# Three edits in a hybrid decoder layer: the w_down sums held until the rotary stage is done, six decay products given more PSUM banks, and the transition to the feed-forward part reordered

## The chip, the cores and the metric

The kernel runs on one core of a Trainium2 chip. The metric is the device time of one execution in microseconds (us); the median of several executions is compared. The engines of the core are TensorE (PE in rows: matmuls; PEld are its weight loads), VectorE (DVE), ScalarE (ACT), GpSimd (POOL) and SyncE (SP, which here only issues DMAs). Each engine works through its instructions in order. PSUM is the memory into which TensorE writes, in banks of 128 x 512 float32.

## What is computed

One layer of a decoder trunk on 1,040 positions (16 meta tokens and 1,024 inputs) of width 1,024, all in float32:

```python
u = rmsnorm(h, mix_norm)
proj = u @ w_in + b_in
aq, ak, av, gq, gk, gv, gr, g_low, gate_a, gate_b = split(proj)
aq, ak = rope(aq), rope(ak)
y_att = swa_attention(aq, ak, av, sinks)          # window of 128, 8 heads, 2 key heads
z = g_low @ w_alpha + b_alpha
log_a = log_sigmoid(z) / 16                       # decay of the linear attention
y_gla = rmsnorm(gla(gq, gk, gv, log_a)) * silu(gr)
h = h + (sigmoid(gate_a) * (y_att @ w_pa) + sigmoid(gate_b) * (y_gla @ w_pg)) @ w_out
u = rmsnorm(h, ffn_norm)
a, v = split(u @ w_up)
h = h + (gelu(causal_dwconv(a)) * v) @ w_down
out = rmsnorm(h, final_norm)[16:]
```

## The kernel before

**Matmuls in two parts.** Every large float32 operand is split into a high part (a cast on ScalarE, L72) and a low part (a subtraction on VectorE, L73). A product is then three matmuls: high x high, high x low, low x high (L91 to L93 in `dense`). A weight strip of 128 columns is loaded by SyncE (L80), split, and used for all positions in three chunks of columns; two strips' buffers alternate.

**Rotary stage.** The loop over j (4 for the keys, then 0 to 3 for the queries) computes a strip q_j, evacuates it on ScalarE into rt (L311, two buffers), copies it with its halves exchanged into rs (L317: four DMAs issued by ScalarE; rs has one buffer), multiplies rs on GpSimd (L318) and rt on VectorE (L319), and adds both into c1 (L330). Behind it come strips gk0, gk1 (keys of the linear attention), gates g0 to g3, gq0, then the first tm weights (token-major products tm0, one for each of nine position tiles, evacuated by VectorE into tv, L385), gq1, the second tm products tm1, and gates from g4 on.

**w_down sums.** The feed-forward products use a seven-product scheme of the Strassen kind, which needs sums of quarter blocks of the weights. For w_down they are made early: `tsum` is a step function that is called between chunks of the projections. Of each three calls one loads a 1 MB block into half of the tile tw (L415), one makes its four sums on VectorE (L421 to L424), and one stores it to the DRAM tile t_d (L418). There are eleven blocks, and tw holds two. Nothing in the data ties these steps to the rotary stage. tw lies in the pool buffer C2, which afterwards holds the tile at of the decay stage (cleared on GpSimd, L473).

**Decay stage.** From the transposed g_low (glT, filled tile by tile through the banks gp) six products z are made (two halves s, three chunks c0; L449), each evacuated twice: by VectorE into zt (L450) and by ScalarE into la (L451). The chain of exp, log and scan behind it ends in the first linear-attention products gm (L483). Banks have tags: "mm" three, "s" two, "pv" two, "pt" one.

**Transition.** The section under `manual_schedule` keeps the written order on its engines; elsewhere a scheduler orders instructions. There the last strip of the output projection (wo7) ends, the root of the mean square is taken for the second half of the positions (nt on TensorE, square root on ScalarE, reciprocal on VectorE, the diagonal matrices dg, and bc, their product with ones), `u2` scales the rows of hT with it (L896), and `op_hi` and `op_lo` split the rows into the operands B22, and after half-subtractions (L1177, L1188, L1191) T1 and T2 (L899, L902). `turn_strip` transposes a strip of hT (th) for its store. `product(n)` does product n of the feed-forward (L978 to L980), for even blocks in two halves of columns; `w_split(n)` makes its weights' parts on ScalarE (L964) and VectorE (L965); `madd` adds a product to an accumulator (L1168).

Of the kernel before, what the change touches and what calls it, by code (L numbers as in the profile page):

```python
# [8 lines left out]
F32 = mybir.dt.float32  # L9
# [37 lines left out]
def hybrid_block(ctx, tc, x, meta, mix_norm, w_in, b_in, w_alpha, b_alpha, sinks, ghn,  # L47
# [9 lines left out]
    def f32(ap):  # L57
        return ap.bitcast(F32)
# [8 lines left out]
    def bank(tag, name):  # L67
        return ps.tile([P, 512], F32, tag=tag, bufs=PB[tag], name=name)
# [337 lines left out]

    t_d = dp.tile([NPAIR, 4, P, 512], F32, name="t_d")
    tw = big.tile([P, 2, 4, 512], F32, tag="C2", name="tw")
    tcount = [0]

    def tsum(c0=0):
# [30 lines left out]
    tq = tm.tile([P, KT * 328], F32R, tag="tl", name="tq")  # L442
    la = f32(tb)[:, :2 * T].rearrange("p (s t) -> p s t", s=2)
    zt = f32(tq)[:, :2 * T].rearrange("p (s t) -> p s t", s=2)
    for s in range(2):
        ba = bcol[:, 29 + s:30 + s]
        for c0, n in CH_ALL:
            o = bank("s", f"z{s}_{c0}")
            pe.matmul(o[:, :n], wal[:, s * P:s * P + P], glT[:, c0:c0 + n], start=True, stop=True)  # L449
            dve.tensor_scalar(zt[:, s, c0:c0 + n], o[:, :n], ba, 0.0, ALU.add, ALU.min)  # L450
            act.activation(la[:, s, c0:c0 + n], o[:, :n], AF.Abs, bias=ba, scale=1.0)  # L451
# [424 lines left out]
    def turn_strip(ht, k, tag="pv"):  # L876
        tp = bank(tag, f"th1_{k}")
        for j in range(4):
            pe.transpose(tp[:, j * P:j * P + P], hT[:, k, 1, 2 + j * P:2 + j * P + P], ident)
        act.copy(ht[:, :, k * P:k * P + P], tp.rearrange("p (j n) -> p j n", j=4))  # L880
        if k % 4 == 3:
            c = k // 4 * 512
            sp.dma_start(h_d[4:8, :, c:c + 512].rearrange("j p n -> p j n"), ht[:, :, c:c + 512])
# [75 lines left out]
    def w_split(n):  # L959
        b, pn = seq[n]  # L960
        nm = SRC[pn]
        src = quarter(b, nm) if nm[0] == "A" else sums[b][nm]
        t = wp.tile([P, 2, 4, P], F32R, tag=("wst", "whi", "wlo")[n % 3], name=f"wq{n}")
        act.copy(t[:, 0], src)  # L964
        dve.tensor_tensor(t[:, 1], src, f32(t[:, 0]), ALU.subtract)  # L965
        slots[n] = t
# [123 lines left out]
    with tc.manual_schedule(engines={mybir.EngineType.PE, mybir.EngineType.DVE, mybir.EngineType.Activation,  # L1090
                                     mybir.EngineType.Pool}):
        wout(6, take("wo6_1"), (2,))
        turn_strip(hts[1], 5)
        w_split(0)
        w_split(3)
        w_last = take("wo7_1")
        w_split(1)
        w_split(2)
        o = dense(w_last, lambda k: mh[k // 4][:, k % 4, 514:1026], lambda k: ml[k // 4][:, k % 4, 514:1026], KT, 512,
                  "wo7_2")  # L1100
        turn_strip(hts[1], 6)
        hv = hT[:, 7, 1, 2:]
        dve.tensor_tensor(hv, hv, o, ALU.add)
        sq = p2.tile([P, 512], F32, tag="sg0", bufs=2, name="sq_last")
        act.activation(sq, hv, AF.Square)
        for b in range(2):
            sum_first(b, 1)
        op_tile(("B22",), big, "C1")
        op_tile(("T2",), big, "C2")
        op_tile(("T1",), b2, "E")  # L1110
        w_split(4)
        w_split(5)
        pr = {0: product(0)}


        nt = bank("pt", "nt")
        for j in range(4):
            pe.matmul(nt[:, j:j + 1], rs[1][:, 2 + j * P:2 + j * P + P], ones_m[:, 0:1], start=True, stop=False)
            pe.matmul(nt[:, j:j + 1], sq[:, j * P:j * P + P], ones_m[:, 0:1], start=False, stop=True)
        act.activation(rt4[:, 0], nt[:, 0:4], AF.Sqrt, bias=eps_c, scale=1.0)  # L1120
        dve.reciprocal(rt4[:, 1], rt4[:, 0])
        dg = p2.tile([P, 4, P], F32, tag="sg1", bufs=2, name="dg")
        for j in range(4):
            if j % 2:
                dve.tensor_scalar(dg[:, j], ident, rt4[:, 1, j:j + 1], None, ALU.mult)
            else:
                act.activation(dg[:, j], ident, AF.Identity, scale=rt4[:, 1, j:j + 1])
        bc = bank("pt", "bc")
        turn_strip(hts[1], 7)

        def spread():
            for j in range(4):
                pe.matmul(bc[:, j * P:j * P + P], ones_f, dg[:, j], start=True, stop=True)

        pr[1] = product(1, spread)
        p1a = b2.tile([P, HQ], F32, tag="rs1", name="p1_0")
        p1v = b2.tile([P, HQ], F32, tag="rs0", name="p1_1")
        keep_prod(0, p1a, pr[0])
        w_split(6)
        pr[2] = product(2)  # L1140
        w_split(7)
        p2.release()
        fp = tc.alloc_tile_pool(name="fp", bufs=1, reuse_waits="tile")
        aa0 = fp.tile([P, 2, HQ], F32, name="aa0")
        vt = fp.tile([P, 4, 4, P], F32, tag="S", bufs=1, name="vt").rearrange("p a k n -> p (a k n)")
        vt = vt[:, 0:1024].rearrange("p (a n) -> p a n", a=2)
        st_load(2)
        st_load(3)
        keep_prod(1, p1v, pr[2])
        pr[3] = product(3)  # L1150

        def lo22(k):
            op_lo("B22", k - 4, 1, hT[:, k:k + 1, 1])

        for k in range(4, 8):
            u2(k, 1, bc)
            op_hi("B22", k - 4, 1, hT[:, k:k + 1, 1])
            if k > 4:
                lo22(k - 1)
        lo22(7)  # L1160
        pr[4] = product(4)
        pr[5] = product(5)

        wk = hT.rearrange("p k h n -> p (k h n)")

        def madd(dst, src, prod, off):
            for o, a, m in prod:
                dve.tensor_tensor(dst[:, a - off:a - off + m], src[:, a - off:a - off + m], o[:, :m], ALU.add)  # L1168

        def half(k, hf):  # L1170
            return hT[:, k:k + 2, hf]

        madd(aa0[:, 0], p1a, pr[1], 0)
        for k in range(4):
            u2(k, 1, bc)
        for k in (0, 2):
            dve.tensor_tensor(half(k, 0), half(k, 1), half(k, 0), ALU.subtract)  # L1177
            op_hi("T1", k, 2, half(k, 0))
        w_split(8)
        for k in (0, 2):  # L1180
            op_lo("T1", k, 2, half(k, 0))
        madd(vt[:, 0], p1v, pr[3], 2)
        pr[6] = product(6)
        pr[7] = product(7)
        keep_prod(0, aa0[:, 1], pr[4])
        keep_prod(1, vt[:, 1], pr[5])
        for k in (0, 2):
            dve.tensor_tensor(half(k, 1), half(k + 4, 1), half(k, 1), ALU.subtract)  # L1188
        op_tile(("T3",), big, "B0")
        for k in (0, 2):  # L1190
            dve.tensor_tensor(half(k + 4, 1), half(k + 4, 1), half(k, 0), ALU.subtract)  # L1191
            op_hi("T2", k, 2, half(k + 4, 1))
        w_split(9)
        for k in (0, 2):
            op_lo("T2", k, 2, half(k + 4, 1))
            op_hi("T3", k, 2, half(k, 1))
        pr[8] = product(8)
        pr[9] = product(9)
        w_split(10)
        w_split(11)  # L1200
        for k in (0, 2):
            op_lo("T3", k, 2, half(k, 1))
        w_split(12)
        w_split(13)
        op_tile(("T4",), big, "B1")
        for k in (0, 2):
            dve.tensor_tensor(half(k + 4, 0), half(k + 4, 0), half(k + 4, 1), ALU.subtract)
            op_hi("T4", k, 2, half(k + 4, 0))
        madd(p1a, p1a, pr[8], 0)
        madd(p1v, p1v, pr[9], 2)  # L1210
        for k in (0, 2):
            op_lo("T4", k, 2, half(k + 4, 0))
        pr[10] = product(10)
        pr[11] = product(11)
        pr[12] = product(12)
        ca, cv, cv0 = whole(0, 1), whole(1, 1), whole(1, 0)
        act.copy(cv0[:, 0], vt[:, 0])
        w_split(14)
        madd(ca[:, 0], p1a, pr[10], 0)
        madd(ca[:, 1], ca[:, 0], pr[6], 0)  # L1220
        madd(aa0[:, 1], aa0[:, 1], pr[6], 0)
        w_split(15)
        pr[13] = product(13)
        madd(cv[:, 0], p1v, pr[11], 2)
        madd(cv[:, 1], cv[:, 0], pr[7], 2)
        madd(cv0[:, 1], vt[:, 1], pr[7], 2)
        sum_make(2)
        dve.tensor_tensor(aa0[:, 1], aa0[:, 1], p1a, ALU.add)
        w_split(16)
        conv(0, 0)  # L1230
        madd(ca[:, 0], ca[:, 0], pr[12], 0)
        conv(0, 1)
        w_split(17)
        dve.tensor_tensor(cv0[:, 1], cv0[:, 1], p1v[:, 0:512], ALU.add)
        madd(cv[:, 0], cv[:, 0], pr[13], 2)
# [215 lines left out]
```

## Time and profile before

| | |
|---|---|
| three runs | 1427.16, 1425.56, 1423.03 us; median 1425.56 |
| profiled execution | 1421.07 us, of which its span (first to last instruction) 1419.3 |
| TensorE | busy 1368.4 us, 96% of the span |
| VectorE, ScalarE, GpSimd | 64%, 41%, 29% |
| mean granted clock of TensorE | 0.983 |

The durations below come from the one profiled execution. The granted clock is given as a share of full speed; its two levels are 1.2 GHz (0.50) and 2.4 GHz (1.00), and a value between them is a mean over a stretch. An engine's idle time costs something only if TensorE waits at the end of it.

### The profile page before, as it was taken

The page shows a single profiled execution, that of the slowest core. Times are in us where ns is not written, and L with a number is a line of the kernel's source. Part 1 is how long each engine was busy: PE and PEld are TensorE (multiplying, and loading weights), DVE is VectorE, ACT ScalarE, POOL GpSimd, SP SyncE. Part 2 cuts the span into 40 slices and gives each one's busy share as a digit, 9 for nine tenths or more (in the row PEclk, how much of TensorE's full clock was granted, in tenths as well). Part 3 has the DMA queues.
Part 4 walks back from the last instruction along what each step waited for, and adds up shares of the span by engine and source line. Part 5 has one row for each costly group of instructions (what it writes and reads, how often), then busy time and mean ns, then how long its engine had stood idle before and what let it go on. Part 6 is the DMA issues. An engine that isn't in the chain of part 4 may idle for free.

```text
span 1419.3 us, 21786 instructions
## 1 busy us (share of the span) xinstructions
PE 1368.4 (96%) x8235; PEld 1244.9 (88%) x8235; DVE 911.1 (64%) x1467; ACT 582.6 (41%) x1145; POOL 416.5 (29%) x289
## 2 busy tenths in 40 slices
PE   6979999989999999999998999999999999999998
PEld 6979999878988988999987888899999888888886
DVE  6566211566677877444467998877676777766674
ACT  6313211535454556443353533333333333654452
POOL 0211110012122221224221387667656652100000
PEclk9989999999999999999999999999999999999999
DMA  7789811122322224555332033233233225975543
GB/s 219 214 250 315 250 44 57 45 71 70 87 70 73 67 73 131 167 168 168 90 134 90 0 127 112 97 112 110 83 112 111 75 97 205 348 262 194 192 151 119
DMA packets 161351, 190.24 MB, mean 134 GB/s; under 512 B 19050, under 2 KB 115110, under 8 KB 161238
## 3 DMA queue, kind: packets, MB, share of 16 engines
q1 hardware_dynamic: 158150, 180.25, 40.4%
q10 hardware_dynamic: 3088, 8.51, 1.9%
q8 instruction: 68, 1.11, 0.3%
q14 instruction: 45, 0.37, 0.1%
HBM read 133.33 MB, written 52.74 MB: 131 GB/s over the span
## 4 chain that ended last, share of the span: by engine, by line
PE 69%; DVE 5%; DMA 2%; ACT 2%; issue 1%; SPq 0%; DVEq 0%; ACTq 0%
PE m L979 10%; PE m L978 10%; PE m L980 10%; PE dn L1376 5%; PE dn L1377 5%; PE dn L1375 5%; PE d_g L91 3%; PE d_g L92 3%; PE d_g L93 3%; PE d_wo L91 2%; PE d_wo L93 2%; PE d_wo L92 2%; PE d_pj L91 2%; PE d_pj L92 2%; PE d_pj L93 2%
## 5 line engine op out<-in xcount | busy, mean ns | idle before, releaser
L979 PE MATMUL m<-op_T,wq 128*128 128x258 f32 (+2 forms) x528 | 170.9, 324 | 5.5 <-DVE op_T L902 5.5
L978 PE MATMUL m<-op_T,wq 128*128 128x258 f32 (+2 forms) x528 | 170.7, 323 | 0.8 <-ACT op_T L899 0.8
L980 PE MATMUL m<-op_T,wq 128*128 128x258 f32 (+2 forms) x528 | 170.1, 322 | 0.0
L91 PE MATMUL d_g<-uh,hi_g 128*128 128x342 f32 x480 | 159.1, 332 | 2.4 <-PEq L571 2.4
L92 PE MATMUL d_g<-ul,hi_g 128*128 128x342 f32 x480 | 156.7, 326 | 2.4 <-issue 2.4
L93 PE MATMUL d_g<-uh,lo_g 128*128 128x342 f32 x480 | 156.5, 326 | 0.0
L979 PE MATMUL m<-op_B,wq 128*128 128x256 f32 (+2 forms) x396 | 127.1, 321 | 0.8 <-DVE op_B L902 0.6
L978 PE MATMUL m<-op_B,wq 128*128 128x256 f32 (+2 forms) x396 | 127.0, 321 | 0.0
L980 PE MATMUL m<-op_B,wq 128*128 128x256 f32 (+2 forms) x396 | 126.4, 320 | 0.0
L979 PEld LDWEIGHTS m<-op_T,wq 128*128 128x128 f32 x528 | 101.3, 192 | 14.1 <-DVE op_T L902 6.4
L964 ACT CAST wq<-S 128x512 fp32r<-128x512 f32 x80 | 49.4, 622 | 148.7 <-PE m L980 127.2
L978 PEld LDWEIGHTS m<-op_T,wq 128*128 128x128 f32 x528 | 101.0, 191 | 9.0 <-ACT op_T L899 1.2
L980 PEld LDWEIGHTS m<-op_T,wq 128*128 128x128 f32 x528 | 101.3, 192 | 7.8
L965 DVE TENSOR_TENSOR wq<-st,wq 128x512 fp32r<-128x512 f32 x72 | 84.8, 1183 | 28.9 <-ACT wq L964 28.9
L91 PEld LDWEIGHTS d_g<-uh,hi_g 128*128 128x128 f32 x480 | 92.7, 193 | 6.4 <-issue 2.8
L93 PEld LDWEIGHTS d_g<-uh,lo_g 128*128 128x128 f32 x480 | 92.7, 193 | 3.2 <-issue 3.1
L92 PEld LDWEIGHTS d_g<-ul,hi_g 128*128 128x128 f32 x480 | 92.8, 193 | 0.5 <-issue 0.4
L1046 POOL TENSOR_TENSOR hT<-hT 128x1024 f32<-128x1024 f32 x22 | 58.8, 2674 | 84.4 <-DVE hT L994 81.9
L979 PEld LDWEIGHTS m<-op_B,wq 128*128 128x128 f32 x396 | 74.9, 189 | 7.2 <-DVE op_B L902 1.2
L978 PEld LDWEIGHTS m<-op_B,wq 128*128 128x128 f32 x396 | 74.8, 189 | 5.8
L980 PEld LDWEIGHTS m<-op_B,wq 128*128 128x128 f32 x396 | 74.8, 189 | 5.8
L965 DVE TENSOR_TENSOR wq<-S,wq 128x512 fp32r<-128x512 f32 x80 | 68.0, 851 | 11.9 <-ACT wq L964 11.2
(345 smaller groups left out, 3682.9 us busy)
## 6 DMA issues: line engine op xcount, KB each, us to landing
st<-in_w_up_dram SPq DMA_DIRECT2D x22, 1024.0 KB, 7.8
stage<-g_d SPq DMA_DIRECT2D x77, 256.0 KB, 4.6
tw<-in_w_down_dram SPq DMA_DIRECT2D x11, 1024.0 KB, 8.4
t_d<-tw SPq DMA_DIRECT2D x11, 1024.0 KB, 5.1
stage<-t_d SPq DMA_DIRECT2D x44, 256.0 KB, 3.5
gate_d<-gev SPq DMA_DIRECT2D x60, 171.0 KB, 2.9
st_g<-in_w_in_dram SPq DMA_DIRECT2D x20, 512.0 KB, 3.8
g_d<-hT SPq DMA_DIRECT2D x11, 768.0 KB, 6.0
```

The source lines that it names most:

```text
L91: pe.matmul(o[:, :n], hi[:, k, :], rh(k), start=(k == 0), stop=False)
L92: pe.matmul(o[:, :n], hi[:, k, :], rl(k), start=False, stop=False)
L93: pe.matmul(o[:, :n], lo[:, k, :], rh(k), start=False, stop=(k == nk - 1))
L964: act.copy(t[:, 0], src)
L965: dve.tensor_tensor(t[:, 1], src, f32(t[:, 0]), ALU.subtract)
L978: pe.matmul(o[:, :m], t[:, 0, k], bh[:, k, a:a + m], start=(k == 0), stop=False)
L979: pe.matmul(o[:, :m], t[:, 0, k], bl[:, k, a:a + m], start=False, stop=False)
L980: pe.matmul(o[:, :m], t[:, 1, k], bh[:, k, a:a + m], start=False, stop=(k == 3))
L1046: pool.tensor_tensor(v, v, wk[:, 1028 + f * 1024:2052 + f * 1024].rearrange("p (h n) -> p h n", h=2), ALU.mult)
L1375: pe.matmul(o, gh[:, ts], dh, start=first, stop=False)
L1376: pe.matmul(o, gh[:, ts], dl, start=False, stop=False)
L1377: pe.matmul(o, gl[:, ts], dh, start=False, stop=last_)
```

## The change

Part A puts two copies of one column from c1, which is complete only after the last rotary add, into the two halves of tw. All loads into tw come after them. Part B takes the banks of the six z from a list. Part C moves the root's work between the two halves of product 0, the transposes of strips 6 and 7 behind product 0, bc ahead of product 1, product 2 forward, u2 and the split of B22 ahead of the weight splits 5, 6 and 7, the half-subtractions ahead of the first `madd`, and the weight splits 8 and 9 behind the second.

```diff
     tw = big.tile([P, 2, 4, 512], F32, tag="C2", name="tw")
+    for z in range(2):
+        dve.tensor_copy(tw[:, z, 0, 0:1], c1[:, 3, 0:1])
     tcount = [0]
...
+    zb = ["s", "pv", "s", "pv", "pt", "s"]
     for s in range(2):
         ba = bcol[:, 29 + s:30 + s]
         for c0, n in CH_ALL:
-            o = bank("s", f"z{s}_{c0}")
+            o = bank(zb.pop(0), f"z{s}_{c0}")
...
-        turn_strip(hts[1], 6)
...
         w_split(4)
-        w_split(5)
-        pr = {0: product(0)}
         nt = bank("pt", "nt")
+        dg = p2.tile([P, 4, P], F32, tag="sg1", bufs=2, name="dg")
+        def roots():
+            for j in range(4):
+                pe.matmul(nt[:, j:j + 1], rs[1][:, 2 + j * P:2 + j * P + P], ones_m[:, 0:1], start=True, stop=False)
+                pe.matmul(nt[:, j:j + 1], sq[:, j * P:j * P + P], ones_m[:, 0:1], start=False, stop=True)
+            act.activation(rt4[:, 0], nt[:, 0:4], AF.Sqrt, bias=eps_c, scale=1.0)
+            dve.reciprocal(rt4[:, 1], rt4[:, 0])
...
+        pr = {0: product(0, roots)}
+        turn_strip(hts[1], 6)
+        turn_strip(hts[1], 7)
+        bc = bank("pt", "bc")
         for j in range(4):
...
-        bc = bank("pt", "bc")
-        turn_strip(hts[1], 7)
-        def spread():
-            for j in range(4):
-                pe.matmul(bc[:, j * P:j * P + P], ones_f, dg[:, j], start=True, stop=True)
-        pr[1] = product(1, spread)
+            pe.matmul(bc[:, j * P:j * P + P], ones_f, dg[:, j], start=True, stop=True)
+        pr[1] = product(1)
...
+        pr[2] = product(2)
+        for k in range(4, 8):
+            u2(k, 1, bc)
+            op_hi("B22", k - 4, 1, hT[:, k:k + 1, 1])
+            if k > 4:
+                lo22(k - 1)
+        lo22(7)
+        w_split(5)
+        for k in range(4):
+            u2(k, 1, bc)
         w_split(6)
-        pr[2] = product(2)
         w_split(7)
...
-        madd(aa0[:, 0], p1a, pr[1], 0)
-        for k in range(4):
-            u2(k, 1, bc)
         for k in (0, 2):
             dve.tensor_tensor(half(k, 0), half(k, 1), half(k, 0), ALU.subtract)
             op_hi("T1", k, 2, half(k, 0))
-        w_split(8)
+        madd(aa0[:, 0], p1a, pr[1], 0)
         for k in (0, 2):
             op_lo("T1", k, 2, half(k, 0))
         madd(vt[:, 0], p1v, pr[3], 2)
+        w_split(8)
+        w_split(9)
...
-        w_split(9)
```

In the changed kernel the lines behind the edits stand two to six lower (L421 is L423, L449 is L452, L896 is L899, L902 is L905, L965 is L968, L1168 is L1174, L1177 is L1180).

VectorE in the rotary stage before (rt0 to rt3 and rs0 to rs3 belong to the four query strips; lo_ names the low part of a weight strip, tw the w_down block):

```order
L319 TENSOR_TENSOR rt0_444<-rt0_444,cs_224 128x1026
L73 TENSOR_TENSOR lo_q3_636<-st_q3_634,hi_q3_635 128x1024
L330 TENSOR_TENSOR c1_428<-rt0_444,rs0_445 128x1026
L421 TENSOR_TENSOR tw_835<-tw_835 128x512
L422 TENSOR_TENSOR tw_835<-tw_835 128x512
L423 TENSOR_TENSOR tw_835<-tw_835 128x512
L319 TENSOR_TENSOR rt1_538<-rt1_538,cs_224 128x1026
L73 TENSOR_TENSOR lo_gk0_730<-st_gk0_728,hi_gk0_729 128x1024
L330 TENSOR_TENSOR c1_428<-rt1_538,rs1_539 128x1026
L424 TENSOR_TENSOR tw_835<-tw_835 128x512
L421 TENSOR_TENSOR tw_835<-tw_835 128x512
L422 TENSOR_TENSOR tw_835<-tw_835 128x512
```

and the same place in the changed kernel:

```order
L73 TENSOR_TENSOR lo_q3_636<-st_q3_634,hi_q3_635 128x1024
L330 TENSOR_TENSOR c1_428<-rt0_444,rs0_445 128x1026
L319 TENSOR_TENSOR rt1_538<-rt1_538,cs_224 128x1026
L73 TENSOR_TENSOR lo_gk0_730<-st_gk0_728,hi_gk0_729 128x1024
L330 TENSOR_TENSOR c1_428<-rt1_538,rs1_539 128x1026
L319 TENSOR_TENSOR rt2_632<-rt2_632,cs_224 128x1026
L73 TENSOR_TENSOR lo_gk1_882<-st_gk1_880,hi_gk1_881 128x1024
L330 TENSOR_TENSOR c1_428<-rt2_632,rs2_633 128x1026
L319 TENSOR_TENSOR rt3_726<-rt3_726,cs_224 128x1026
L73 TENSOR_TENSOR lo_g0_966<-st_g0_964,hi_g0_965 128x1024
L330 TENSOR_TENSOR c1_428<-rt3_726,rs3_727 128x1026
L410 COPY tw_835<-c1_428 128x1 x2
```

The sums that stood between the rotary operations stand behind the last of them, and behind the new copies; all other rows keep their order.

TensorE in the decay stage before (z0 and z1 are the two halves, the number behind is the chunk; gp8 is the last transpose of g_low; d_g4 is gate strip g4):

```order
L394 MATMUL gp8_2251<-ident_73,tv1_8_2248 16x128
L449 MATMUL z0_0_2256<-glT_831,wal_829 128x272
L449 MATMUL z0_272_2260<-glT_831,wal_829 128x384
L93 MATMUL d_g4_14_2319<-uh_78,lo_g4_1880 128x342
L91 MATMUL d_g4_14_2319<-uh_78,hi_g4_1879 128x342
L92 MATMUL d_g4_14_2319<-ul0_79,hi_g4_1879 128x342
L93 MATMUL d_g4_14_2319<-uh_78,lo_g4_1880 128x342
L449 MATMUL z0_656_2264<-glT_831,wal_829 128x384
L91 MATMUL d_g4_14_2319<-uh_78,hi_g4_1879 128x342
L449 MATMUL z1_0_2268<-glT_831,wal_829 128x272
L92 MATMUL d_g4_14_2319<-ul0_79,hi_g4_1879 128x342
L93 MATMUL d_g4_14_2319<-uh_78,lo_g4_1880 128x342
```

and in the changed kernel, from the end of the last tm product on:

```order
L452 MATMUL z0_272_2262<-glT_831,wal_829 128x384
L452 MATMUL z1_0_2270<-glT_831,wal_829 128x272
L394 MATMUL gp8_2253<-ident_73,tv1_8_2250 16x128
L452 MATMUL z0_0_2258<-glT_831,wal_829 128x272
L452 MATMUL z0_656_2266<-glT_831,wal_829 128x384
L452 MATMUL z1_272_2274<-glT_831,wal_829 128x384
L452 MATMUL z1_656_2278<-glT_831,wal_829 128x384
L91 MATMUL d_g4_14_2321<-uh_78,hi_g4_1881 128x342
L92 MATMUL d_g4_14_2321<-ul0_79,hi_g4_1881 128x342
L93 MATMUL d_g4_14_2321<-uh_78,lo_g4_1882 128x342
```

The six z, which were spread among matmuls of g4, stand in one run ahead of g4, with gp8 among them.

VectorE in the transition before (wq4 to wq8 are the weight splits of products 4 to 8; op_B22 and op_T1 are low parts of operands; aa0 is the first madd):

```order
L1121 RECIPROCAL rt4_115<-rt4_115 128x4
L1125 TENSOR_SCALAR dg_8719<-ident_73,rt4_115 128x128 x2
L965 TENSOR_TENSOR wq6_8766<-s1t_8246,wq6_8766 128x512
L965 TENSOR_TENSOR wq7_8782<-s1t_8246,wq7_8782 128x512
L896 SCALAR_TENSOR_TENSOR hT_6649<-hT_6649,ccol_104,bc_8724 128x512 x2
L902 TENSOR_TENSOR op_B22_8673<-hT_6649,op_B22_8673 128x514
L896 SCALAR_TENSOR_TENSOR hT_6649<-hT_6649,ccol_104,bc_8724 128x512
L902 TENSOR_TENSOR op_B22_8673<-hT_6649,op_B22_8673 128x514
L896 SCALAR_TENSOR_TENSOR hT_6649<-hT_6649,ccol_104,bc_8724 128x512
L902 TENSOR_TENSOR op_B22_8673<-hT_6649,op_B22_8673 128x514 x2
L1168 TENSOR_TENSOR aa0_8789<-p1_0_8762,m1_0_8732 128x258
L1168 TENSOR_TENSOR aa0_8789<-p1_0_8762,m1_258_8749 128x256
```

and in the changed kernel from the reciprocal on:

```order
L1124 RECIPROCAL rt4_115<-rt4_115 128x4
L1127 TENSOR_SCALAR dg_8676<-ident_73,rt4_115 128x128 x2
L899 SCALAR_TENSOR_TENSOR hT_6651<-hT_6651,ccol_104,bc_8730 128x512 x2
L905 TENSOR_TENSOR op_B22_8669<-hT_6651,op_B22_8669 128x514
L899 SCALAR_TENSOR_TENSOR hT_6651<-hT_6651,ccol_104,bc_8730 128x512
L905 TENSOR_TENSOR op_B22_8669<-hT_6651,op_B22_8669 128x514
L899 SCALAR_TENSOR_TENSOR hT_6651<-hT_6651,ccol_104,bc_8730 128x512
L905 TENSOR_TENSOR op_B22_8669<-hT_6651,op_B22_8669 128x514 x2
L968 TENSOR_TENSOR wq5_8790<-st01_8247,wq5_8790 128x512
L899 SCALAR_TENSOR_TENSOR hT_6651<-hT_6651,ccol_104,bc_8730 128x512 x4
L968 TENSOR_TENSOR wq6_8797<-s1t_8248,wq6_8797 128x512
L968 TENSOR_TENSOR wq7_8800<-s1t_8248,wq7_8800 128x512
```

The splits wq6 and wq7, and wq5 (which stood just before the reciprocal), are now behind the low parts of B22. Behind the rows of the second list follow the half-subtractions, aa0, the low parts of T1, vt, and only then wq8 and wq9.

## Rows read from the trace of the kernel before

**Rows 1.** waits of TensorE over the whole span: us in total, times, longest
```profile
PE m L979 <- DVE op_T L902: 5.5, 3, 3.1
...
PE gm L483 <- DVE tq L496: 1.5, 2, 0.9
```

**Rows 2.** timeline of VectorE: start, us, line, op, out<-in [idle before <-releaser]
```profile
77.13 0.69 DVE L421 TENSOR_TENSOR tw<-tw 128x512 f32<-128x512 f32 x1 [10.62 <-DMA tw<-in_w_down_dram]
...
83.55 1.22 DVE L330 TENSOR_TENSOR c<-rt,rs 128x1026 f32<-128x1026 f32 x1
```

**Rows 3.** timeline of ScalarE, rotary stage; ACTq is its queue, here issuing copies
```profile
84.85 4.28 ACTq L317 DMA_DIRECT2D rs<-rt  x4
89.18 1.42 ACT L311 ACTIVATE rt<-d_q,ccol 128x258 f32<-128x258 f32 x3 [17.58 <-DMA rs<-rt]
...
101.29 2.45 ACTq L317 DMA_DIRECT2D rs<-rt  x4
```

**Rows 4.** timeline of GpSimd, rotary stage
```profile
95.60 3.40 POOL L318 TENSOR_TENSOR rs<-rs,sn 128x1026 f32<-128x1026 f32 x1 [15.51 <-DMA rs<-rt]
106.97 3.40 POOL L318 TENSOR_TENSOR rs<-rs,sn 128x1026 f32<-128x1026 f32 x1 [7.98 <-DMA rs<-rt]
```

**Rows 5.** timeline of TensorE, first matmuls of gk0 and of tm_0
```profile
89.71 0.59 PE L91 MATMUL d_gk<-uh,hi_gk 128*128 128x272 f32 x1 [8.36 <-ACT rt L311]
...
171.94 0.31 PE L381 MATMUL tm<-th,uh 128*16 128x328 f32 x1
```

**Rows 6.** table by stretches; columns stand in its first line
```profile
core 0: us, PE busy (x) PEld busy (x) DVE busy (x) ACT busy (x) POOL busy (x), PEclk, DMA share, GB/s
90.00:100.00 10.00, 10.00 (x52) 10.00 (x52) 4.50 (x2) 2.02 (x4) 3.40 (x1) 0.75 1.00 338
120.00:140.00 20.00, 20.00 (x129) 20.00 (x129) 10.90 (x18) 9.93 (x17) 0.00 (x0) 1.00 1.00 314
180.00:200.00 20.00, 20.00 (x136) 20.00 (x135) 2.50 (x5) 2.62 (x14) 4.17 (x14) 1.00 0.10 32
```

**Rows 7.** timeline of SyncE's queue, rotary stage
```profile
85.40 3.15 SPq L418 DMA_DIRECT2D t_d<-tw  x2
```

**Rows 8.** issues of the w_down loads: min/median/max, first and last start
```profile
L415 SPq DMA_DIRECT2D tw<-in_w_down_dram x11: 367/451/1155, 39.1 to 157.6; - x11
...
DMA to landing us min/median/max: 6.1/8.4/10.7
```

**Rows 9.** timeline of TensorE, decay products
```profile
251.00 1.37 PE L449 MATMUL z<-glT,wal 16*128 16x272 f32 x4
...
256.29 2.92 PE L449 MATMUL z<-glT,wal 16*128 16x384 f32 x4
```

**Rows 10.** table by stretches, decay products (columns as in rows 6)
```profile
255.00:256.00 1.00, 1.00 (x6) 0.92 (x5) 0.50 (x1) 0.70 (x2) 0.00 (x0) 0.74 0.00 0
256.00:262.00 6.00, 6.00 (x16) 4.01 (x15) 1.24 (x2) 2.75 (x5) 0.00 (x0) 0.50 0.01 3
```

**Rows 11.** timeline of VectorE, transition to feed-forward
```profile
758.10 1.40 DVE L896 SCALAR_TENSOR_TENSOR hT<-hT,ccol,bc 128x512 f32<-128x512 f32 x2
...
771.92 0.69 DVE L965 TENSOR_TENSOR wq<-st,wq 128x512 fp32r<-128x512 f32 x1 [1.63 <-ACT wq L964]
772.53 2.36 DVE L902 TENSOR_TENSOR op_T<-hT,op_T 128x1028 fp32r<-128x1028 f32 x2
...
809.63 0.68 DVE L965 TENSOR_TENSOR wq<-S,wq 128x512 fp32r<-128x512 f32 x1
```

**Rows 12.** timeline of TensorE, transition to feed-forward
```profile
752.74 0.36 PE L978 MATMUL m<-op_B,wq 128*128 128x258 f32 x1
...
754.26 1.05 PE L1133 MATMUL bc<-dg,ones_f 128*128 128x128 f32 x8
...
773.81 0.39 PE L979 MATMUL m<-op_T,wq 128*128 128x258 f32 x1 [3.14 <-DVE op_T L902]
...
811.23 0.28 PE L980 MATMUL m<-op_T,wq 128*128 128x258 f32 x1
```

More of the change, by code (lines that the diff above doesn't have):

```diff
@@ L1111, in hybrid_block @@
         w_split(4)
-        w_split(5)
-        pr = {0: product(0)}
         nt = bank("pt", "nt")
-        for j in range(4):
[L1118 to L1122, printed above, removed]
-        for j in range(4):
[L1124 to L1127, printed above, removed]
-        bc = bank("pt", "bc")
-        turn_strip(hts[1], 7)
-        def spread():
-            for j in range(4):
-                pe.matmul(bc[:, j * P:j * P + P], ones_f, dg[:, j], start=True, stop=True)
-        pr[1] = product(1, spread)
+        dg = p2.tile([P, 4, P], F32, tag="sg1", bufs=2, name="dg")
[5 more added lines that the diff above has]
+            dve.reciprocal(rt4[:, 1], rt4[:, 0])
+            for j in range(4):
+                if j % 2:
+                    dve.tensor_scalar(dg[:, j], ident, rt4[:, 1, j:j + 1], None, ALU.mult)
+                else:
+                    act.activation(dg[:, j], ident, AF.Identity, scale=rt4[:, 1, j:j + 1])
+        pr = {0: product(0, roots)}
+        turn_strip(hts[1], 6)
+        turn_strip(hts[1], 7)
+        bc = bank("pt", "bc")
+        for j in range(4):
+            pe.matmul(bc[:, j * P:j * P + P], ones_f, dg[:, j], start=True, stop=True)
+        pr[1] = product(1)
         p1a = b2.tile([P, HQ], F32, tag="rs1", name="p1_0")
@@ L1138, in hybrid_block, with lo22 @@
         keep_prod(0, p1a, pr[0])
+        pr[2] = product(2)
+        def lo22(k):
+            op_lo("B22", k - 4, 1, hT[:, k:k + 1, 1])
+        for k in range(4, 8):
[7 more added lines that the diff above has]
+            u2(k, 1, bc)
         w_split(6)
-        pr[2] = product(2)
         w_split(7)
@@ L1150, in hybrid_block @@
         pr[3] = product(3)
-        def lo22(k):
-            op_lo("B22", k - 4, 1, hT[:, k:k + 1, 1])
-        for k in range(4, 8):
-            u2(k, 1, bc)
[L1157 to L1160, printed above, removed]
         pr[4] = product(4)
@@ L1171, in half @@
             return hT[:, k:k + 2, hf]
-        madd(aa0[:, 0], p1a, pr[1], 0)
-        for k in range(4):
-            u2(k, 1, bc)
         for k in (0, 2):
```

## The prediction

> **What bounds the kernel now.** TensorE is busy 96% of the span (table above), so only places where it waits or runs at its lower clock can give time back. I read first its waits, summed by releaser [rows 1]: 5.5 us in three pieces, the longest 3.1, for the low parts of a feed-forward operand (L902), and 1.5 in the decay stage (L483); and one of 8.36 for ScalarE's rotary evacuation L311 [rows 5]. They lie in the three stretches that the change touches. Then I followed each stretch engine by engine, and last read the granted clock around it.
>
> *Rotary stretch.* The 8.36 us stand before the first matmul of strip gk0, at 89.71 [rows 5]. The releaser is the ScalarE group at 89.18, which itself sat 17.58 us until a rotary copy had landed [rows 3]. Why was it late? VectorE waited 10.62 us for a w_down block at 77.13; the rotary add behind it came at 83.55 [rows 2], and as rs has one buffer, the next copy was issued only at 84.85. GpSimd had it at 95.60, 10.75 us later; the copy issued at 101.29 was there at 106.97, 5.7 us later [rows 3, 4]. Beside the slow copy two stores of 1 MB ran, issued at 85.40 [rows 7], and two loads behind them. A rotary round is copy, product on GpSimd (3.4) and add (1.2): 15.3 us with a slow copy, 10.3 with a fast one. TensorE does 129 matmuls in 20 us [rows 6], so a strip of 72 in 11.2. A slow round is late, a fast one isn't. Behind the stall the clock is 0.75 of full over 90 to 100 us [rows 6]: 10 x 0.25 = 2.5 us more.
>
> **A, w_down sums behind the rotary stage.** Gone from VectorE between rotary operations: the wait of 10.62 and six groups of four sums (0.7 each); gone from the DMA engines before about 96 us: six loads and their stores. Rounds then take about 10.3 against 11.2, so gk0 should follow q3 without a stall: −8.4, and −2.5 for the clock. Added: two copies of one column, bounded by nothing and by a whole sum (0.7) each. I take nothing: VectorE idles in this stretch, and without that cover they delay only the sums behind them.
>
> What is late next? The last rotary add stands behind g0's weight split on VectorE, and that split needs gk0's buffer. gk0 ends near 89.71 − 8.4 + 11.2 = 92.5; cast, split and add bring 96, the first load goes out about 98. Behind its wait on SyncE stand tm and strip weights. Seven sum groups now stand in front of the first tv evacuation, so I checked their pace. Loads 3 to 7 stand on SyncE between the gate stores of g0 to g3, one or two loads a strip, which puts load 7 near 150; with 8.4 to landing [rows 8] and four sums of 0.7 its group is done near 162. TensorE wants the bank of tm_0 back after three tm products of 24 x 20/136 = 3.5 us [rows 6], at 171.94 + 10.6 − 10 = 172.5 [rows 5]: 10 us of margin. The last store ends near 200, far ahead of the decay stage (first product at 251 [rows 9]), which overwrites the buffer. The eleventh group (2.8 us) now stands among the splits of the second tm weights: between 0 and 2.8 given back. I take 0.8, nearer nothing, because VectorE was busy for only 2.50 of 20 us beside the tm products [rows 6]. **A: −10.1** (bounds −5, the slow-copy rival, and −10.9).
>
> **B, banks of the decay products.** Before, six z share two banks and wait for each other's evacuation; TensorE fills in with g4's matmuls between them. It shows work in all 6.00 us from 256 to 262, at a granted clock of 0.50, and at 0.74 in the us before [rows 10]: 3.0 + 0.3 = 3.3 us lost. Afterwards the six stand in one run ahead of g4; at 1.37 us for 656 of 2080 columns [rows 9] that is 4.3 us, ending near 255.3 where now the last four passes end at 256.29 + 2.92 = 259.2. What the clock does then no row shows: it may fall for as long (gain 0) or not at all (3.3). I take half, 1.7, as it fell here only after z's and g4 had alternated for several us. The decay chain behind starts 3.9 earlier; the gm waits of 1.5 lie at its end, but some of their work has other inputs: between 0 and 1.5 I take 0.9. **B: −2.6** (bounds 0 and −4.8).
>
> The Trainium skill, "TensorE: Matmul & The Clock Gate", Part 1 (what's actually happening), says that the clock is set by how busy TensorE has been lately, the low rate being for idle. By it alone a gap-free run of z keeps the clock, B is −4.2 and the sum 1.6 lower. The row of 6 busy us at 0.50 doesn't agree with the plain reading of it.
>
> **C, transition.** Roots go between the halves of product 0, bc goes ahead of product 1, and u2 of the second half no longer stands behind three weight splits. Before, TensorE did product 1's first half from 752.74 and bc from 754.26, for 1.05 [rows 12]; u2 began at 758.10 [rows 11]. After, that half stands behind bc, so bc can end at 755.31 − 1.52 = 753.8; its inputs come from nt, which starts earlier by th_6 and half a product and so isn't late. The hand-overs between three engines I put at 0.5: u2 at 754.3, 3.8 earlier. From u2 to T1's low parts (772.53) VectorE took 14.4 us [rows 11]. Into this stretch move the three splits that stood in front of it, 2.1; out of it goes split 8, 0.7, with the wait of 1.63 for its cast [rows 11]: 14.2. T1's low parts start at 768.5, 4.0 earlier. Splits 8 and 9, put behind them, cost nothing here, as VectorE already stood idle for ScalarE's casts there.
>
> TensorE waited 3.14 us for that low part at 773.81 [rows 12], 5.5 in all three places; its own path would gain that much. But it can't gain more than what feeds it later: the split of product 17 ended at 809.63 + 0.68 = 810.31 [rows 11] and was first used at 811.23 [rows 12], a slack of 0.92. So at most 4.0 + 0.9 = 4.9; at least 4.0 − 2.4 = 1.6, if T1's low parts have to wait for a pair of casts as long as themselves (2.36). I take 4.6, near the cap because the waits alone exceed it. **C: −4.6** (−1.6 to −4.9).
>
> **Sum.** −10.1 − 2.6 − 4.6 = −17.3: the profiled execution's 1421.07 becomes 1403.8. It lies 4.5 below the median of the runs, 1425.56, so the forecast of the median is 1425.56 − 17.3 = **1408**.
>
> **The rivals.**
> *Small B and C.* The clock falls for as long in the z stage, and casts delay T1: 10.1 + 1.6 = 11.7, 1414. For it: ScalarE makes those casts beside evacuations of products; against: it is busy 41%.
> *The copies stay slow.* If strip loads and not w_down's slow them, rounds stay at 15.3, 4.1 over a strip; the 10.62 wait goes, but a stall of 4 to 5 with half of the clock loss stays. A is −5, the sum −12.2: 1413. Against: the copy of 5.7 had a strip load beside it.
> *All in full.* 10.9 + 4.8 + 4.9 = 20.6: 1405. The rule on the clock leads this way.
> *Slower: moved sums pile up in front of tv_0.* VectorE is in order, so if the seventh group is late, tv_0 is, and TensorE stands for a bank. With P us a round, group 7 ends at 98 + 6P + 11.2 against 172.5, so it bites above P = 10.5; groups 8 to 10 stand among eight tm products of 3.5 and cost 3P − 28 more. Before, eleven loads went out from 39.1 to 157.6 [rows 8], 11.85 a round, and the DMA engines were busy all of 120 to 140 [rows 6]. At 11.85 the loss is 15 and the change gains 2; at 12.1 it gains nothing; at 13 it loses 8: 1434. Against: that pace was set by the places in the program where the steps are called; after the hold-back they are overdue.
>
> The Trainium skill, "Trainium Kernel Development and Optimization", Best Practices, advises to overlap DMA with compute by double buffers, which speaks against holding loads back and leads to this rival. In this trace the overlap goes with the copies of 10.75 us, and the loads have time later.
>
> **How the numbers follow.** Chances: the forecast 0.63, small B and C 0.13, slow copies 0.08, all in full 0.11, slower 0.05. The likeliest one's own range is 1405 to 1412; the range that leaves out no more than 2 in 10 takes in the neighbours and the spread of single executions: **1402 to 1416**. A measurement of this kernel tells about 0.3%, 4.3 us, from no change (three runs of before spread by 4.1). Of the 0.95 that end lower I give 0.05 to slow copies together with small B and C, or a pile-up near 12: faster 0.90, same 0.05, slower 0.05.
>
> **What would show it.** A: TensorE's wait for L311 gone, copies near 6 us before 98, clock full from 80 to 100, gk0's first matmul near 81; w_down loads from 98 on, last store near 200, no wait of tm products for tv. B: six z in one run of 4 to 5 us, low clock for 3 us or less, gm waits under 1. C: u2 earlier by 4 beyond A and B, the waits for op_T's low parts under 1.5 in all, product 17 waiting less than 1. The forecast is wrong if TensorE waits for the bank of tm_0, if a copy still takes 10 us, or if VectorE's waits for ScalarE's casts grow in the transition.

## The result, and the profile after

The changed kernel took 1409.85 us (median of four runs, 1408.20 to 1413.57), the kernel before beside it 1424.30 (four runs). The ratio is 0.9897, 95% interval 0.9873 to 0.9921: 11 to 18 us faster. The forecast was 1408. The profiled executions are 1408.20 and 1421.07, with spans of 1406.4 and 1419.3, 12.9 apart.

To see where the time went I matched the matmuls of two traces one by one and took the difference of their starts. The table has this shift at the ends of six stages, each less the one at the stage's start (us, minus is earlier). The last column is the forecast.

| stage, up to | part | after | forecast |
|---|---|---|---|
| first tm matmul (171.94 before) | A | −11.6 | −10.9 |
| last matmul of the second tm products (249.81) | A, given back | +6.4 | +0.8 |
| first gm (277.68) | B | −2.9 | −2.6 |
| last matmul of the output projection (747.12) | untouched | +1.6 | 0 |
| a third into the feed-forward products (829.46) | C | −6.0 | −4.6 |
| last matmul (1412.11) | untouched | −0.5 | 0 |
| sum | | −12.9 | −17.3 |

So the time was met, but by errors of both signs: A gave back 6.4 instead of 0.8, and C brought more than the upper bound it was given. That the total came out so close is in part luck.

**Rotary stage.** The copy that ScalarE issued last, in the timeline of the changed kernel:

```profile
84.95 2.44 ACTq L317 DMA_DIRECT2D rs<-rt  x4
```

and GpSimd's products on the copies:

```profile
68.15 3.47 POOL L318 TENSOR_TENSOR rs<-rs,sn 128x1026 f32<-128x1026 f32 x1 [7.99 <-DMA rs<-rt]
79.25 3.39 POOL L318 TENSOR_TENSOR rs<-rs,sn 128x1026 f32<-128x1026 f32 x1 [7.64 <-DMA rs<-rt]
90.31 3.47 POOL L318 TENSOR_TENSOR rs<-rs,sn 128x1026 f32<-128x1026 f32 x1 [7.67 <-DMA rs<-rt]
```

84.95 to 90.31 is 5.4 us, where [rows 3, 4] had 10.75. TensorE starts gk0 with no wait:

```profile
80.61 0.29 PE L91 MATMUL d_gk<-uh,hi_gk 128*128 128x272 f32 x1
```

The table by stretches shows full clock where it was 0.75 [rows 6] (the lower two lines belong to the next two paragraphs):

```profile
core 0: us, PE busy (x) PEld busy (x) DVE busy (x) ACT busy (x) POOL busy (x), PEclk, DMA share, GB/s
80.00:90.00 10.00, 10.00 (x66) 10.00 (x65) 2.89 (x3) 2.59 (x4) 2.65 (x1) 1.00 0.41 107
90.00:100.00 10.00, 10.00 (x66) 10.00 (x64) 3.81 (x5) 2.52 (x4) 3.68 (x2) 1.00 0.31 84
...
209.00:217.00 8.00, 7.58 (x32) 5.86 (x33) 3.28 (x6) 3.03 (x6) 3.52 (x1) 0.60 0.79 242
249.00:253.00 4.00, 4.00 (x16) 3.98 (x16) 0.64 (x2) 3.77 (x4) 0.00 (x0) 0.57 0.02 4
```

**Second tm weights.** TensorE's waits after; the L311 wait [rows 5] is gone, the 5.5 us for op_T's low parts [rows 1] are 1.2, the gm wait is as it was, and lines for tm are new:

```profile
PE tm L381 <- ACT th L72: 1.5, 1, 1.5
PE gm L486 <- DVE tq L499: 1.5, 2, 0.9
...
PE m L982 <- DVE op_T L905: 1.2, 3, 0.9
...
PE tm L382 <- DVE tl L73: 0.9, 2, 0.5
```

These waits are short, yet 6.4 us went. In order of time, TensorE:

```profile
206.26 0.32 PE L382 MATMUL tm<-tl,uh 128*16 128x328 f32 x1 [0.47 <-DVE tl L73]
...
207.27 0.32 PE L382 MATMUL tm<-tl,uh 128*16 128x328 f32 x1 [0.39 <-DVE tl L73]
...
209.26 0.46 PE L381 MATMUL tm<-th,uh 128*16 128x328 f32 x1 [1.52 <-ACT th L72]
```

It waits 0.47, 0.39 and 1.52 us, and the granted clock is 0.60 over 209 to 217 (table above): 8 x 0.40 = 3.2 us. Waits of 2.4 us and these 3.2 make 5.6 of the 6.4; the experiments below come back to how the two go together. What was late? ScalarE's third cast of these weights, VectorE's eleventh group of sums, and, in SyncE's queue, the loads (tst) behind stores of tv and the last w_down load:

```profile
204.56 0.87 ACT L72 CAST th<-tst 128x328 fp32r<-128x328 f32 x2 [7.16 <-DMA tst<-in_w_in_dram]
```

```profile
203.65 0.69 DVE L423 TENSOR_TENSOR tw<-tw 128x512 f32<-128x512 f32 x1 [6.35 <-DMA tw<-in_w_down_dram]
```

```profile
195.18 0.36 SPq L420 DMA_DIRECT2D t_d<-tw  x1
195.63 0.58 SPq L388 DMA_DIRECT2D gv_d<-tv  x1
196.30 1.14 SPq L417 DMA_DIRECT2D tw<-in_w_down_dram  x1
197.54 1.12 SPq L388 DMA_DIRECT2D gv_d<-tv  x1
198.71 0.50 SPq L370 DMA_DIRECT2D tst<-in_w_in_dram  x1
```

The lateness can be followed step by step. Before, the first cast, the load for the third cast, the third cast itself and the last cast of these weights ran at

```profile
204.45 0.83 ACT L72 CAST th<-tst 128x328 fp32r<-128x328 f32 x2 [2.60 <-PE tm L383]
205.47 0.35 SPq L370 DMA_DIRECT2D tst<-in_w_in_dram  x1
208.07 0.47 ACT L72 CAST th<-tst 128x328 fp32r<-128x328 f32 x1
217.60 0.47 ACT L72 CAST th<-tst 128x328 fp32r<-128x328 f32 x1 [0.38 <-DMA tst<-in_w_in_dram]
```

and after, with the tenth block's sums in front of them, the first cast ran at

```profile
192.28 0.69 DVE L423 TENSOR_TENSOR tw<-tw 128x512 f32<-128x512 f32 x1 [3.38 <-DMA tw<-in_w_down_dram]
195.59 0.39 ACT L357 CAST vs<-tv 128x64 fp32r<-128x64 f32 x2 [6.27 <-DVE tv L385]
195.89 0.83 ACT L72 CAST th<-tst 128x328 fp32r<-128x328 f32 x2
```

Less the shift of −11.6, the first cast is 3.0 us late, because the last tv stand behind the tenth block's sums on VectorE, and ScalarE's casts of tv ahead of its cast of the weights. The load for the third cast is 4.8 late, as it also stands in SyncE's queue, and the third cast 8.1, as its load took 5.8 us to its use instead of 2.6. The last low part of these weights is 8.1 us late.

The w_down loads as a whole, answering to [rows 8]:

```profile
L417 SPq DMA_DIRECT2D tw<-in_w_down_dram x11: 368/379/1143, 100.9 to 196.3; - x11
```

They went out from 100.9 to 196.3, 9.5 us a round; the prediction had the first at 98 and the last store near 200, which was issued at 208.2.

**Decay products.** The six z stand in one run, 4.2 us with a gp between:

```profile
244.85 1.37 PE L452 MATMUL z<-glT,wal 16*128 16x384 f32 x4
...
246.35 2.74 PE L452 MATMUL z<-glT,wal 16*128 16x272 f32 x8
```

Then the clock falls all the same, to 0.57 over 249 to 253 (table above), so for about 3.5 us at half instead of about 7.

**Transition.** VectorE starts u2 at 747.70, B22's first low part right behind the first pair, and T1's low parts at 760.44:

```profile
747.70 1.41 DVE L899 SCALAR_TENSOR_TENSOR hT<-hT,ccol,bc 128x512 f32<-128x512 f32 x2 [2.10 <-PE bc L1136]
749.14 0.69 DVE L905 TENSOR_TENSOR op_B<-hT,op_B 128x514 fp32r<-128x514 f32 x1
...
760.44 2.36 DVE L905 TENSOR_TENSOR op_T<-hT,op_T 128x1028 fp32r<-128x1028 f32 x2
```

Against [rows 11], and with TensorE's shift of 6.4 up to there taken off, u2 is 4.0 us earlier (forecast 3.8), T1's low parts 5.7 (forecast 4.0).

### The profile page after: what moved, and what is told of

It is laid out like the page before. It is cut to its first block, busy times and chain, and to the rows that moved or that the text cites. A ratio compares the mean times of both kernels' runs of the same rounds, so it can differ in the third digit from the quotient of the medians.

```text
span 1406.4 us, 21784 instructions
## 1 busy us (share of the span) xinstructions
PE 1365.6 (97%) x8235; PEld 1243.3 (88%) x8235; DVE 904.0 (64%) x1469; ACT 583.2 (41%) x1145; POOL 417.9 (30%) x289
## 4 chain that ended last, share of the span: by engine, by line
PE 68%; DVE 7%; ACT 2%; issue 1%; DMA 1%; POOL 0%; SPq 0%; DVEq 0%; ACTq 0%; POOLq 0%
PE m L981 9%; PE m L982 9%; PE m L983 9%; PE dn L1380 5%; PE dn L1381 5%; PE dn L1379 5%; PE d_g L91 3%; PE d_g L93 3%; PE d_g L92 3%; PE d_wo L91 2%; PE d_pj L91 2%; PE d_pj L92 2%; PE d_pj L93 2%; PE d_wo L92 2%; PE d_wo L93 2%
## 5 line engine op out<-in xcount | busy, mean ns | idle before, releaser
L968 DVE TENSOR_TENSOR wq<-st,wq 128x512 fp32r<-128x512 f32 x72 | 84.4, 1178 | 25.8 <-ACT wq L967 25.8
L668 POOL TENSOR_TENSOR pr<-pr,mkn 128x512 fp32r<-128x512 f32 x16 | 26.8, 1673 | 164.1 <-DVE pr L662 142.7
```

## The experiments

**The parts alone.** Each is the kernel before with the edits of that part.

> Part A alone. Theory 1 (read from the two traces): the rotary stage ends 11.6 us earlier, and about 6 us are given back where the second tm weights are split, because the eleventh w_down block lands behind them: -5 to -6 us in all (ratio 0.996). Theory 2 (the give-back belongs to another part of the change or to chance): A keeps its 11 us (ratio 0.992).

> Part B alone. Theory 1: the six z run in one row and save 2.9 us around the stage, nothing at the gm products: -3 us (ratio 0.998). Theory 2: the gain in the changed kernel came from where the clock stood after A's shift and not from the banks: 0 to -1 us.

> Part C alone. Theory 1: VectorE's chain through T1's low parts is 5.5 us earlier (4 from u2, 1.5 from the waits for casts of B22 that go), TensorE gains 6 to 7 us (ratio 0.9955). Theory 2 (the cap of the prediction holds, the rest of the gain was chance): -4.6 us (ratio 0.997).

Measured: A alone 0.9977 (0.9957 to 0.9997), B alone 0.9985 (0.9969 to 1.0001), C alone 0.9969 (0.9952 to 0.9986). By stages of the traces: A −10.0 to the first tm matmul and +6.1 behind it; B −1.3; C −5.9. A and C each do in their own stage nearly what they do in the whole change, and theory 2 of A and of C falls; B's stage shows less than half of its 2.9 (why is said further down). B alone can't be told from no change by its time. The product of the three ratios is 0.993 against 0.9897 of the whole; with an interval of about ±0.002 on each of the four, this difference is no more than scatter can give.

**Release one or two outputs earlier.** The copies into tw read another column block:

```diff
-        dve.tensor_copy(tw[:, z, 0, 0:1], c1[:, 3, 0:1])
+        dve.tensor_copy(tw[:, z, 0, 0:1], c1[:, 2, 0:1])    # rel_j1: c1[:, 1, 0:1]
```

> The whole change, but the copies into tw wait for the third rotary output (j = 2) and not the last. Theory 1 (the give-back is lateness of the last w_down blocks): loads begin about 12 us earlier, near 87, the eleventh lands before the second tm weights are split, and 5 to 6 us more are gained than by the change (about 1404); the last rotary copy may be slow again, but TensorE doesn't wait for it. Theory 2 (slow copies cost TensorE whenever a load runs beside any of them): a stall before gk0 or gk1 comes back and it is no faster than the change (1410 or more).

> The whole change, the copies into tw wait for the second rotary output (j = 1) only. Theory 1 (before, the stall in front of gk0 came from several slow rounds in a row together with VectorE's waits for w_down blocks): loads start near 74, the copies of j = 2 and 3 take near 10 us instead of 5.5, but the evacuation of q3 needs only the buffer of j = 1, so gk0 starts within 1 us of the changed kernel. Theory 2 (one slow copy is enough): a stall of 2 to 5 us in front of gk0 or gk1. At the second tm weights 1 to 4 us come back, as the blocks end some 15 us earlier.

rel_j2: 1414.16 us, 0.9933 (0.9912 to 0.9955), not the 1404 that I expected, and by its interval not clearly other than the changed kernel. Its loads:

```profile
L417 SPq DMA_DIRECT2D tw<-in_w_down_dram x11: 372/383/579, 85.1 to 183.3; - x11
```

The blocks end 13 us earlier, no sum stands among the second tm weights any more, and still 3.8 us are given back up to the end of the tm products, beside 2.1 less gain before: the theory that the eleventh block's lateness is all falls. VectorE's last tv, ahead of the low parts, waited here 4.74 us for a store of tv. No stall came back in front of gk0 or gk1, so theory 2 doesn't hold either. rel_j1 (one run, 1417.76 beside 1423.58): gk0 starts in time, as theory 1 has it, but GpSimd gets the copies late,

```profile
103.91 2.65 POOL L318 TENSOR_TENSOR rs<-rs,sn 128x1026 f32<-128x1026 f32 x1 [14.80 <-DMA rs<-rt]
```

and VectorE, in order, stands 7.79 us for a w_down block in front of that block's sums, the rotary product (L319) and g0's weight split (L73, at 108.89):

```profile
103.64 0.69 DVE L423 TENSOR_TENSOR tw<-tw 128x512 f32<-128x512 f32 x1 [7.79 <-DMA tw<-in_w_down_dram]
```

TensorE waits for this split instead.

```profile
PE d_g L93 <- DVE lo_g L73: 4.6, 1, 4.6
```

The split stands ahead of the rotary add that needs the slow copy, so what costs here is VectorE's wait for the block, not the copy. Up to the first tm matmul this kernel gained only 2.4.

**The eleventh block without its sums, without its load.** Both leave out part of w_down's sums, and each ran once (1405.46 and 1407.63 us beside a median of 1425.18 before).

```diff
-        elif r == 2 and i < NPAIR:          # no_sum11; no_load11: the same bound at r == 0
+        elif r == 2 and i < NPAIR - 1:
```

> The whole change without the four sums of the eleventh w_down block (its load and store stay). Theory 1 (VectorE's in-order wait for the late eleventh block holds up the second tm weights): the second tm products start 5 to 6 us earlier against the first ones than in the changed kernel. Theory 2 (the moved blocks' transfers and SyncE's queue hold up the tv stores and the loads of the second tm weights): at most 1 to 2 us come back, as the load is still there; ScalarE still waits for tst before the third cast.

> The whole change without the load of the eleventh w_down block (its sums run on the ninth block's old contents, its store stays). Theory 1: the same 5 to 6 us come back as without the sums. Theory 2: more than without the sums, 2 to 4 us, because one of the last transfers is gone; the stores in front of it remain.

Given back in the tm stage: 3.8 without the sums, 7.5 without the load, 6.4 in the changed kernel; five executions of kernels with part A as it is there gave 6.1 to 10.4. Neither theory fits. Without the sums ScalarE still waits for the third weight block:

```profile
202.47 0.90 ACT L72 CAST th<-tst 128x328 fp32r<-128x328 f32 x2 [5.81 <-DMA tst<-in_w_in_dram]
```

(204.56 in the changed kernel). Without the load, the eleventh block's sums stand right behind the tenth's, which waited 4.04 us for their block, and still ahead of the last tv.

The loss goes, roughly, with how late the last low part of these weights comes. The table has this lateness, against the first tm matmul and the kernel before, for every trace with a hold (us); beside it TensorE's waits in the stage, and what the lower clock took there, which is half of the time at half clock. (The changed kernel's 2.6 are the 2.4 above and 0.2 for a tv.)

| kernel | last low part late | waits | clock | given back |
|---|---|---|---|---|
| rel_j2 | 3.8 | 2.5 | 0 | 3.8 |
| rel_j1 | 5.0 | 4.5 | 0 | 5.0 |
| no_sum11 | 6.1 | 2.3 | 1.7 | 3.8 |
| no_load11 | 6.3 | 4.4 | 3.4 | 7.5 |
| changed kernel | 8.1 | 2.6 | 3.4 | 6.4 |
| A alone | 8.2 | 3.5 | 1.7 | 6.1 |
| c_evac | 9.4 | 4.1 | 3.4 | 7.1 |
| c_root_only | 9.8 | 4.1 | 1.7 | 7.4 |
| c_late_root | 12.4 | 6.6 | 3.4 | 10.4 |
| late3 | 0.3 | 0.8 | 0 | 1.0 |
| late4 | 0.1 | 0.7 | 0 | 0.6 |

The changed kernel and A alone are equally late and give back about the same, one with more of it in the clock, the other in waits: a likely reading is that at the lower clock TensorE comes later to weights for which it would else wait. So the clock is not shown to be a second loss on top. Each leave-out made the last low part some 2 us less late than in the changed kernel, which the spread of single executions (8.1 to 12.4 with the same A) doesn't let one call a gain.

**The last blocks held a second time.** In late3 and late4 the last three or four blocks wait for the last low part of the second tm weights:

```diff
     w1 = tm_weights(1)
+    for z in (0, 1):                       # late4: (1, 0)
+        dve.tensor_copy(tw[:, z, 0, 0:1], f32(w1[1][:, 7, 0:1]))
+        if z == 0:                         # late4: z == 1
+            tsum()
+            tsum()
...
-            tsum()
+            if hf or i < 6:                # late4: i < 3
+                tsum()
```

> The whole change, with the last three w_down blocks held a second time, until the last low part of the second tm weights is made. Both theories give the 5 to 6 us back, as neither sums nor transfers of these blocks lie in front of the second tm weights any more: a ratio of about 0.986 against the kernel before (1404 to 1405). If instead the eight blocks in front are enough to slow the stores of tv (a third theory), half of it or less comes back. The three late blocks should end near 245, before the decay stage needs their buffer near 265.

> As the run before with four late blocks. By theory 1 no further gain (0 to 0.5 us). By theory 2 and the third theory 0.5 to 2 us more, since one transfer fewer lies beside the first tm products. If the last store is late for the clearing of at, GpSimd's wait for it shows in the gm products: +1 to +5.

late3: 1405.69 us, 0.9867 (0.9838 to 0.9896); late4: 1403.48 us, 0.9850 (0.9825 to 0.9876), the lowest median here. Their intervals overlap, and late4's just overlaps that of the changed kernel (from 0.9873); the clear evidence is in the stage itself. Given back in the tm stage: 0.96 and 0.56. The 0.4 between the two fits theory 1 (0 to 0.5), and is too little to tell the theories apart. In late4 the third cast comes 2.5 us after its load was issued, against 5.8 in the changed kernel:

```profile
197.67 0.47 ACT L72 CAST th<-tst 128x328 fp32r<-128x328 f32 x1
```

```profile
195.13 0.36 SPq L370 DMA_DIRECT2D tst<-in_w_in_dram  x1
```

and the clock stays at 1.00 in 209 to 217, while the DMA engines, nearly idle before [rows 6] and here over 180 to 200, do the late blocks (columns as in the table above):

```profile
180.00:200.00 20.00, 20.00 (x137) 20.00 (x136) 4.17 (x9) 4.11 (x15) 3.47 (x11) 1.00 0.19 50
209.00:217.00 8.00, 8.00 (x54) 7.58 (x53) 2.37 (x4) 0.42 (x2) 0.00 (x0) 1.00 0.94 322
244.00:250.00 6.00, 6.00 (x19) 4.87 (x18) 1.24 (x2) 4.74 (x5) 1.41 (x1) 0.50 0.01 3
```

No gm product is late for it. This settles the place: the last three or four rounds of blocks lay on the path to the second tm weights. No run separates the shares; the trace of the changed kernel puts, of the third cast's 8.1 us, 3.0 to the order on VectorE and ScalarE, 1.8 to SyncE's queue and 3.3 to the slower load.

**The transition taken apart.** Each of these three ran once (c_late_root 1416.09, c_root_only 1420.03, c_evac 1419.44 us, beside 1423.58 before). c_late_root puts root, transposes and bc back to their old places; c_root_only keeps them early with the old order of u2, splits and product 2; c_evac moves one line of ScalarE:

```diff
         pr[2] = product(2)
+        keep_prod(1, p1v, pr[2])
...
-        keep_prod(1, p1v, pr[2])
         pr[3] = product(3)
```

> The whole change, but product 2 is evacuated by ScalarE right behind its issue, ahead of the casts of B22, as before the change. Theory 1 (the part of C's gain that the prediction missed is ScalarE's in-order wait for product 2 in front of these casts): the casts start only when product 2 ends, near 753.5 instead of 748.5, T1's low parts come 3 to 5 us later than in the changed kernel, and most of C's 6.7 us is lost. Theory 2 (the gain comes from u2's earlier start alone): no change of more than 0.5 us in the transition.

> The whole change with root, transposes and bc at their old places (bc between the halves of product 1), the new order of u2, splits and evacuations kept. Theory 1: u2 starts 1 to 1.5 us later than in the changed kernel, and the transition takes 1 to 1.5 us more. Theory 2 (the early root is the gain): 3 to 4 us more.

> The whole change with the early root, but u2, splits 5 to 9, the first madd and product 2 in the old order. Theory 1: VectorE still stands at the splits 6 and 7, whose casts wait for products 0 and 1 to free their buffers; u2 starts about as late as in the kernel before, and 5 to 6 of C's 6.7 us are lost. Theory 2: 3 us or less are lost.

The stage gained 6.0 in the whole change (5.9 to 6.0 in all eight traces that have C), 4.8 with the late root, 0.6 with the early evacuation, −0.7 with the early root alone. Theory 1 holds in all three. (The expectations put C's gain at 6.7; between the table's ends it is 6.0.) In c_evac ScalarE, in order, waits 5.39 us for product 2 in front of the casts of B22, and VectorE for them:

```profile
757.57 0.59 ACT L1004 COPY p<-m 128x512 f32<-128x512 f32 x1 [5.39 <-PE m L983]
```

```profile
758.71 0.70 DVE L905 TENSOR_TENSOR op_B<-hT,op_B 128x514 fp32r<-128x514 f32 x1 [5.42 <-ACT op_B L902]
```

In c_root_only VectorE still stands at splits 6 and 7 before u2:

```profile
754.64 0.69 DVE L968 TENSOR_TENSOR wq<-s1t,wq 128x512 fp32r<-128x512 f32 x1 [2.27 <-ACT wq L967]
757.13 0.69 DVE L968 TENSOR_TENSOR wq<-s1t,wq 128x512 fp32r<-128x512 f32 x1 [1.80 <-ACT wq L967]
757.74 0.74 DVE L899 SCALAR_TENSOR_TENSOR hT<-hT,ccol,bc 128x512 f32<-128x512 f32 x1
```

## Why the prediction was right, and where it was wrong

*A, the stall.* Right by its mechanism: copies of 5.4 us, rounds of 11.1 (68.15, 79.25, 90.31; 10.3 was forecast, and a strip takes TensorE 11.2), no stall, full clock. −8.4 − 2.5 was −11.6, and −10.0 to −11.5 in the other traces with A as it is here. Part A takes away both the slow copies and VectorE's waits for w_down blocks; how the stall was shared between them no run shows, and in rel_j1 it was the second that cost.

*A, what is late next.* The step in front of tv_0 was rightly put: the seventh group ended at 166.2 (forecast 162), tv_0 ran right behind it, and TensorE waited 0.2 us for a tv. The rival's wait is not far, though: in c_late_root, with the same part A, TensorE waited 1.2 and 2.3 us for a tv behind such sums. The failed step is the next: the eleventh group "between 0 and 2.8", 0.8 taken, because VectorE had been nearly idle there. It measured 6.4 up to the end of the tm products, and the lateness began one group earlier, with the tenth. Idle time of the engine in the trace of before said nothing, as loads, casts and splits form a chain whose end had no slack already then: the last cast began at 217.60 (above), and TensorE, which began these products at 215.72, used the last low part at 219.03. Behind such a chain a wait of any engine in it counts. The rival named the pile-up but looked for it only in front of tv_0.

*B.* 2.9 for 2.6 in this execution, but the 0.9 for gm was wrong: the gm wait is 1.5 in every trace. And the gain is not one number. Eleven traces have part B: its stage gained 1.3 in four, in which the clock was at half for about 7 us as before the change, 2.8 to 2.9 in six with about 3.5 us of it, 4.4 in one. So the clock brought 0, 1.5 or 3.1. Of the 1.3 that stay, 0.3 is a wait in front of the first gm that the trace of before shows and no other; the rest stays open. The trace with 4.4 is no_load11, in which the clock did not fall:

```profile
247.00:252.00 5.00, 5.00 (x22) 3.18 (x21) 3.35 (x6) 3.77 (x8) 0.00 (x0) 1.00 0.09 32
```

In late4 it was at 0.50 over 244 to 250 (table above). All of them have the same run of z. The bounds that the prediction set for the clock, no fall and a full fall, were both met, and that half of it was met in the changed kernel is luck.

The Trainium skill, "TensorE: Matmul & The Clock Gate", Part 1 (what's actually happening), says that at a kernel's start the number of matmuls at the low rate varies from run to run. Here, from kernel to kernel, the time at the low rate in the middle varies too: 0, about 3.5 and about 7 us behind the same z. By its rule that a busy TensorE keeps the clock no fall was expected; that holds in one trace of eleven.

*C.* u2's start was right to 0.2 us. The step that was mis-sized is "from u2 to T1's low parts 14.2": it was 12.7. The ledger counted splits, but not the 1.2 us in which VectorE waited for B22's first cast, because ScalarE stood at the evacuation of product 2, as the trace of before has it:

```profile
759.58 0.59 ACT L1001 COPY p<-m 128x512 f32<-128x512 f32 x1 [2.12 <-PE m L980]
760.72 0.69 DVE L902 TENSOR_TENSOR op_B<-hT,op_B 128x514 fp32r<-128x514 f32 x1 [1.22 <-ACT op_B L899]
```

Moving product 2's evacuation behind the casts is part of the change, and c_evac shows that without this one move 5.4 of the 6.0 are lost. The cap was right as a mechanism (product 17's split came 5.5 earlier, with its 0.9 of slack 6.4, and 6.0 was gained), only the chain in it was too short.

*The untouched stages* moved by +1.6 and −0.5 in this execution; over all traces the middle stage moved by −1.0 to +7.3 (the last in C alone, whose trace has more stretches at the lower clock there); what those falls follow I did not look into. The single profiled execution is good to some us, the stages with waits to some tenths.

## What to carry to other kernels

When loads are held back to clear a stage, follow them to where they end: price the last ones, not only the first, against the tightest chain of loads, casts and splits that follows, and give the tail a second release behind that chain. An engine's idle time does not say that a chain through it has slack; the time between its last output and the first use does. On engines that work in order look for an evacuation in front of a cast: one line's place was worth 5.4 us here. Before a fall of the clock is counted on top of waits, compare with a kernel whose inputs are equally late.

## What the runs showed of the hardware that was not expected

Waits far shorter than the stretch behind them can go with a fall of the clock, and need not. In the changed kernel 2.4 us of waits were followed by 0.60 over 209 to 217; in rel_j2 2.3 us of waits between 209 and 214, in six pieces of up to 0.98, were followed by none (1.00 over 209 to 217 and 217 to 225). The same run of six small products was followed by 0, about 3.5 or about 7 us at half clock in different kernels' traces, though TensorE shows work in all of these stretches. A load of 128 x 312 values took 2.5 us to its use in late4, with the DMA engines at 0.19 over 180 to 200, and 5.8 in the changed kernel beside a 1 MB store and a 1 MB load issued 3.5 and 2.4 us before it.
